# The experts' weights laid out as pieces, two pieces to a tile and to a DMA

## The chip, the cores and the metric

The program runs on one core of one Trainium2 chip. The metric is the device time of one execution in microseconds (us). The kernel before took 1800.74 us, the median of three runs (1800.19 to 1805.48 us).

## What is computed

Three transformer blocks run one after the other on 256 tokens of width 1024, all in float32. The change is in the second layer of the second block, a mixture of experts: a router picks two of eight experts for each token, and each expert is a SwiGLU with a hidden width of 2816.

```python
def expert_block(args):
    xb, e = args
    return (jax.nn.silu(xb @ w1[e]) * (xb @ w3[e])) @ w2[e]
...
contrib = y_sorted * gate_flat[order][:, None].astype(h.dtype)
out = jax.ops.segment_sum(contrib, sorted_token, num_segments=n_tok)
```

Here `w1[e]` and `w3[e]` are 1024 x 2816 and `w2[e]` is 2816 x 1024, so the eight experts hold 277 MB of weights. Every other stage (attention of several kinds, two dense SwiGLUs, a gated mixer, embeddings per layer) also multiplies the activations by weights that are read once from DRAM.

## The kernel before, in words

**Pieces.** Every weight matrix passes through the chip in pieces of 128 partitions by 1024 float32 (512 KB, 4 KB in a partition). `K.load` (L623) takes a raw buffer in turn from the list `s.raws` and issues one DMA on the SP queue (L632). `K.split` (L636) then makes two fp32r tiles of the raw piece: ScalarE copies it to `hi` (L649), and VectorE writes `lo = raw - hi` (L650). TensorE multiplies three times per product (`mm3`, L673): high by high, high by low and low by high (L675 to L677). The raw buffer is free again when L650 has read it. There are four `hi` and four `lo` buffers (`NH`).

**Rows of a piece.** A piece of an expert's `w1` or `w3` is two blocks of 128 rows by 512 columns (rows of 2 KB in DRAM), or, in the last group of an expert, four blocks by 256 columns (rows of 1 KB). A piece of `w2` is 128 rows of 1024 columns (4 KB). An expert has 66 pieces, all eight 528.

**Raw buffers.** All stages share eight raw buffers of 4 KB a partition (`s.wr`, `NR = 8`); some stages (`phase(..., raw=n)`, L526) add some of their own. Stage `block2b` (L1398) has a ring of ten more for its mixer and the experts. For the experts the list of raw buffers is then made 25 long: these 18, the buffer `xw`, four halves of the two tiles Yh and Yl (class `Spare`, L475), `xt`, and one of the four tiles `b4`. One further piece goes once into another `b4` tile (`units.where`).

**Order of the experts.** `Units` (L411) lists all pieces in the order in which they are taken: a group's `w1` and `w3`, then the `w2` of the group before. `Units.ahead` loads a piece early, `Units.fetch` splits the next one (and loads it if it was not loaded), `Units.take` hands it to `experts` (L1590). Pieces 0 to 2 are fetched and 3 to 7 loaded ahead in `gm` (L1444), the stage before; pieces 4 to 7 go to `b4` tiles. In `route`, `experts` and around them the order of TensorE, VectorE and ScalarE is written out by hand (`with s.in_order()`, L546). In the other stages, and on the SP queue, the builder of the program orders the instructions by priorities and by a model of time of its own, so they need not follow the code.

**After the experts.** `moe` (L1535) loads the eight pieces of `ple_gate` into the eight buffers `s.wr`, reads a count, and branches (`tc.If(cnt > P)`, L1545) around a second pass over all experts, which is needed only if an expert has over 128 tokens. In these runs the branch is not taken into the second pass.

Of the kernel before, what the change touches and what calls it, by code (L numbers as in the profile page):

```python
# [9 lines left out]
F32 = mybir.dt.float32  # L10
# [9 lines left out]
P = 128  # L20
D = 1024
NEG = -1.0e30
FF = 2816
NE = 8
# [53 lines left out]
    return pk  # L78


def host_layout(I):

    return {
        "final_gain": I["final_gain"].reshape(1, D),
        "final_norm_2": I["final_norm_2"].reshape(1, D),
        "final_norm_g_3": I["final_norm_g_3"].reshape(1, D),
        "ln_ffn1": I["ln_ffn_2"][1:2],
        "c_ln_g_2": I["c_ln_g_2"].reshape(1, D),
        "c_ln_b_2": I["c_ln_b_2"].reshape(1, D),
        "c_w_sT": np.ascontiguousarray(I["c_w_s_2"][0].transpose(2, 0, 1)),  # L90
        "positions_2": np.ascontiguousarray(I["positions_2"].reshape(2, P).T),
    }
# [86 lines left out]
class NextX:  # L179
# [5 lines left out]
    def __init__(s, k, g, row, tag, width, off):  # L185
        s.k, s.row, s.off = k, row, off
        s.pair = k.x_pair(tag, [P, 8, width])
        s.ssq = k.ts(8)
        if row is None:
            s.g = g  # L190
        else:
            s.grow = k.bcast(row)
            s.g = k.ts(8)
            k.nc.vector.tensor_tensor(out=s.g, in0=k.p(row), in1=g, op=ALU.mult)
# [54 lines left out]
class Last:  # L249
# [7 lines left out]
    def half(s, t):  # L257
# [11 lines left out]
        nc.vector.scalar_tensor_tensor(h[:, t, cs[1]], h[:, t, cs[1]], r, s.grow[:, cs[1]], op0=ALU.mult, op1=ALU.mult)  # L269
        out = k.A["out"].rearrange("(t p) d -> p t d", p=P)  # L270
        for c in cs:
# [139 lines left out]
class Units:  # L411


    def __init__(s, k):
        A = k.A
        s.k, s.early, s.where, s.n, s.loaded, s.ready = k, {}, {}, 0, 0, []
        s.todo = []
        todo2 = []
        for e in range(NE):
            for g0 in range(0, FF // P, 4):  # L420
                n = min(4, FF // P - g0)
                for w in ("moe_w1_2", "moe_w3_2"):
                    s.todo += [(src, kp, n * P, c) for c, src, kp in k.pieces(A[w][0, e], 0, 8, g0 * P, n * P)]
                s.todo += todo2
                todo2 = [(src, kp, D, g0 + c) for c, src, kp in k.pieces(A["moe_w2_2"][0, e], g0, n, 0, D)]
        s.todo += todo2

    def load(s, n, pool=None):
        src, kp, w, _ = s.todo[n]
        s.loaded = max(s.loaded, n + 1)  # L430
        return s.k.load(src, kp, w, None if pool is None else pool.tile([P, D], F32, tag="raw", name=s.k.nm("raw")))

    def ahead(s, n, pool=None):
        s.early[n] = s.load(n, pool)

    def fetch(s):

        if s.n < len(s.todo):
            hi, lo = s.k.split(*(s.early.pop(s.n, None) or s.load(s.n, s.where.get(s.n))))
            _, kp, _, c = s.todo[s.n]  # L440
            s.ready.append([(c + j, hi[:, j], lo[:, j]) for j in range(kp)])
            s.n += 1

# [16 lines left out]
class InTurn:  # L460
# [5 lines left out]
    def tile(s, shape, dt, tag, name):  # L466
        s.pools.append(s.pools.pop(0))
        return s.pools[-1].tile(shape, dt, tag="one", name=name)

    def keep(s):  # L470

        s.pools.pop()


class Spare:  # L475


    def __init__(s, k):
        s.k, s.n = k, 0

    def tile(s, shape, dt, tag, name):
        if s.n % 2 == 0:
            s.t = s.k.xp.tile([P, 2 * D], F32, tag="Y" + "hl"[s.n // 2 % 2], name=name)
        s.n += 1
        return s.t[:, :D] if s.n % 2 else s.t[:, D:]


class K:
    UE = 1024

    def __init__(s, ctx, tc, A):
        s.tc, s.nc, s.A = tc, tc.nc, A
        pool = lambda name, bufs, **kw: ctx.enter_context(tc.tile_pool(name=name, bufs=bufs, **kw))
        nc = s.nc
        s.n = 0
        s.cp = pool("cp", 1)
        s.NR, s.NH = 8, 4
        s.wr, s.wh, s.wl = pool("wr", s.NR), pool("wh", s.NH), pool("wl", s.NH)
        s.xp = pool("xp", 1)

        s.sm = pool("sm", 48)
        s.dp = pool("dp", 1, space=DRAM)
        s.ct, s.chain = {}, (None, {})
        s.h = s.cp.tile([P, 2, D], F32, name="h")
        x = A["x"].rearrange("(t p) d -> p t d", p=P)
        ck = s.cp.tile([P, C_W["ck"]], F32, name="ck")
        s.ct["ck"] = ck
        nc.sync.dma_start(ck[:, :P], A["ck"][:, :P])
        for i in range(2):
            for t in range(2):  # L510
                nc.sync.dma_start(s.h[:, t, 512 * i:512 * i + 512], x[:, t, 512 * i:512 * i + 512])
        s.pk = s.cp.tile([P, PK_2], F32, name="pk")
        nc.sync.dma_start(s.pk[:, :PK_1], A["pk"][:, :PK_1])
        s.ident = s.c("ident")
        s.later = True
# [6 lines left out]
            s.later = False  # L522


    @contextmanager
    def phase(s, name, b8=0, b4=0, b2=0, b1=0, raw=0, hl=0, ring=None, ps=(("mm", 4), ("acc", 2), ("fil", 2)), extra=()):  # L526
        with ExitStack() as st:
            pool = lambda nm, bufs, **kw: st.enter_context(
                s.tc.tile_pool(name=f"{name}_{nm}", bufs=bufs, reuse_waits="tile", **kw))
            s.b8 = pool("b8", b8) if b8 else None  # L530
            s.b4 = pool("b4", b4) if b4 else None
            s.b2 = pool("b2", b2) if b2 else None
            s.b1 = pool("b1", b1) if b1 else None
            s.one = pool("one", 1)
            for nm, bufs in extra:
                setattr(s, nm, pool(nm, bufs))
            mk = lambda base, n, nm, m: [base] * n + ([pool(nm, m)] * m if m else [])
            s.raws, s.his, s.los = mk(s.wr, s.NR, "xr", raw), mk(s.wh, s.NH, "xh", hl), mk(s.wl, s.NH, "xl", hl)
            if ring is not None:
                s.raws = s.raws + [ring[0]] * ring[1]  # L540
            s.nraw = s.nhl = 0
            s.psp = ps if isinstance(ps, dict) else {t: pool(f"ps_{t}", n, space=PSUM) for t, n in ps}
            yield

# [853 lines left out]
    def block2b(s):  # L1398
        with ExitStack() as st:
            pool = lambda nm, bufs, **kw: st.enter_context(s.tc.tile_pool(name="b2b_" + nm, bufs=bufs, **kw))  # L1400
            ring, kp = pool("xr", 10), pool("pp", 1)
            b4 = [pool(f"b4{i}", 1, reuse_waits="tile") for i in range(4)]
            xw, xt = pool("xw", 1), pool("xt", 1)
            keep = lambda shape, dt=F32: kp.tile(shape, dt, name=s.nm("keep"))
            pq = InTurn([pool("pq", 1, reuse_waits="tile")])
            ps = [pool(f"ps{i}", 1, space=PSUM, reuse_waits="tile") for i in range(8)]
            with s.phase("gm", b8=2, b2=2, ring=(ring, 10), ps=dict(mm=InTurn(ps[:4]), acc=InTurn(ps[4:6]), fil=InTurn(ps[6:]))):
                s.b4 = InTurn(b4)
                s.consts("cm", kp)

                nc = s.nc
                nc.gpsimd.memset(keep([P, 72]), 0.0)
                t = xt.tile([P, 4, 256], F32R, tag="raw", name=s.nm("pT"))
                pT = s.ple_in(1, (t[:, 0:2], t[:, 2:4]))
                units, rest, pp = s.gm(pT, pq, keep, xw.tile([P, 8, 128], F32, tag="raw", name=s.nm("wst")))
                at = s.nraw % len(s.raws)
                raws = s.raws[at:] + s.raws[:at] + [xw] + [Spare(s)] * 4 + [xt, InTurn(b4[2:3])]
            with s.phase("moe", b1=3, ps=dict(mm=InTurn(ps[:2]), ab=InTurn(ps[2:6]), acc=InTurn(ps[6:])), extra=(("bx", 4),)):
                s.raws = raws
                s.sh, s.hp, s.yp = [InTurn([b4[i]]) for i in (0, 1, 3)]  # L1420

                units.where = {units.loaded + len(raws): s.yp}
                s.b4 = InTurn(b4)
                nx, pre = s.moe(units, ring, rest)
                s.b4 = InTurn(b4)
                s.x3()
                s.b4 = InTurn(b4[1:])
                s.ple(1, nx, pp, s.x, pre, ("acc", "ab"))
# [566 lines left out]
def build(tc, A, phases):  # L1995
    with ExitStack() as ctx:
        k = K(ctx, tc, A)
        for ph in phases:
# [2 lines left out]

PHASES = ("block1", "block2a", "block2b", "block3")
DIRECT = ("w_in_even", "w_out_even", "w_in_odd", "w_out_odd", "p_2", "a_w_in_2", "a_w_out_2", "ffn_w1_2", "ffn_w3_2",
          "ffn_w2_2", "c_w_in_2", "c_w_out_2", "moe_w1_2", "moe_w3_2", "moe_w2_2", "ple_gate_2", "ple_proj_2",
          "meta_tokens_3", "w_in_3", "w_uq_3", "w_ukv_3", "w_o_3", "w_gate_3", "w_up_3", "w_down_3")


# [22 lines left out]
```

## Time and profile before

| | before |
|---|---|
| three runs | 1800.19, 1800.74, 1805.48 us |
| the profiled execution | 1804.6 us |
| its span, first to last instruction | 1802.8 us |
| mean granted TensorE clock | 0.991 |
| bytes read from DRAM | 443.61 MB |
| experts' DMAs | 528 of 512 KB |

The profiled execution took 1.8 us more than its span, and 3.9 us more than the median of the three runs. An engine is busy while it works on an instruction that is no wait, branch or DMA issue. PE is TensorE's matmuls and PEld its weight loads, DVE is VectorE, ACT ScalarE, POOL GpSimd, SP the engine whose queue issues the DMAs. Matmuls overlap each other in the records, so their distance is read from their starts.

### The profile page before, as it was taken

The page shows a single profiled execution, that of the slowest core. Times are in us where ns is not written, and L with a number is a line of the kernel's source. Part 1 is how long each engine was busy: PE and PEld are TensorE (multiplying, and loading weights), DVE is VectorE, ACT ScalarE, POOL GpSimd, SP SyncE. Part 2 cuts the span into 40 slices and gives each one's busy share as a digit, 9 for nine tenths or more (in the row PEclk, how much of TensorE's full clock was granted, in tenths as well). Part 3 has the DMA queues.
Part 4 walks back from the last instruction along what each step waited for, and adds up shares of the span by engine and source line. Part 5 has one row for each costly group of instructions (what it writes and reads, how often), then busy time and mean ns, then how long its engine had stood idle before and what let it go on. Part 6 is the DMA issues. An engine that isn't in the chain of part 4 may idle for free. (4 is left out here: it accounts for less than half of the span.)

```text
span 1802.8 us, 27631 instructions
## 1 busy us (share of the span) xinstructions
PE 1770.3 (98%) x10129; PEld 1536.7 (85%) x10129; DVE 1389.0 (77%) x2013; ACT 1136.2 (63%) x1566; POOL 92.5 (5%) x102
## 2 busy tenths in 40 slices
PE   8999999999999999999999999999999899999998
PEld 7879879899987888888888888888888688889997
DVE  6676779745466789998989999999999788865544
ACT  6354665644456568777777787777878665554443
POOL 1100010111000110000000000000000020001101
PEclk9899999999999999999999999999999899999999
DMA  8535463866547879999999999999997554357640
GB/s 285 192 118 163 146 193 127 262 183 186 186 139 246 278 249 372 354 365 341 363 366 359 359 344 377 347 379 320 379 355 275 163 161 132 94 191 219 187 130 24
DMA packets 215761, 446.57 MB, mean 248 GB/s; under 512 B 15145, under 2 KB 44081, under 8 KB 215489
## 3 DMA queue, kind: packets, MB, share of 16 engines
q1 hardware_dynamic: 215616, 444.72, 72.5%
q8 instruction: 81, 1.33, 0.3%
q14 instruction: 64, 0.52, 0.1%
HBM read 443.61 MB, written 2.63 MB: 248 GB/s over the span
## 5 line engine op out<-in xcount | busy, mean ns | idle before, releaser
L650 DVE TENSOR_TENSOR lo<-raw,hi 128x1024 fp32r<-128x1024 f32 (+1 forms) x828 | 989.0, 1225 | 303.8 <-ACT hi L649 292.8
L649 ACT CAST hi<-raw 128x1024 fp32r<-128x1024 f32 (+1 forms) x828 | 851.9, 1048 | 443.4 <-PE mm L677 134.0
L675 PE MATMUL ab<-hi,bx 128*128 128x512 f32 (+1 forms) x768 | 290.6, 378 | 0.0
L676 PE MATMUL ab<-hi,bx 128*128 128x512 f32 (+1 forms) x768 | 285.7, 372 | 0.3 <-DVE bx L746 0.3
L677 PE MATMUL ab<-lo,bx 128*128 128x512 f32 (+1 forms) x768 | 286.0, 372 | 0.0
L675 PE MATMUL mm<-Xh,hi 128*128 128x256 f32 x760 | 215.7, 284 | 2.0 <-DVE Xl L749 2.0
L677 PE MATMUL mm<-Xl,hi 128*128 128x256 f32 x760 | 215.4, 283 | 0.0
L676 PE MATMUL mm<-Xh,lo 128*128 128x256 f32 x760 | 215.3, 283 | 0.0
L677 PEld LDWEIGHTS ab<-lo,bx 128*128 128x128 f32 x768 | 144.6, 188 | 25.7
L676 PEld LDWEIGHTS ab<-hi,bx 128*128 128x128 f32 x768 | 144.9, 189 | 24.3 <-DVE bx L746 0.6
L675 PEld LDWEIGHTS ab<-hi,bx 128*128 128x128 f32 x768 | 144.8, 189 | 23.7
L675 PEld LDWEIGHTS mm<-Xh,hi 128*128 128x128 f32 x760 | 146.0, 192 | 3.2 <-ACT hi L649 2.3
L676 PEld LDWEIGHTS mm<-Xh,lo 128*128 128x128 f32 x760 | 146.0, 192 | 0.9 <-DVE lo L650 0.2
L677 PEld LDWEIGHTS mm<-Xl,hi 128*128 128x128 f32 x760 | 146.1, 192 | 0.0
L675 PE MATMUL acc<-hi,hp 128*128 128x512 f32 x352 | 137.3, 390 | 0.0
L676 PE MATMUL acc<-hi,hp 128*128 128x512 f32 x352 | 137.1, 390 | 0.0
L677 PE MATMUL acc<-lo,hp 128*128 128x512 f32 x352 | 137.0, 389 | 0.0
L675 PE MATMUL fil<-Xh,hi 128*128 128x256 f32 (+1 forms) x352 | 102.4, 291 | 1.0 <-ACT b L1919 0.5
L677 PE MATMUL fil<-Xl,hi 128*128 128x256 f32 (+1 forms) x352 | 101.0, 287 | 0.0
L676 PE MATMUL fil<-Xh,lo 128*128 128x256 f32 (+1 forms) x352 | 100.9, 287 | 0.0
L677 PEld LDWEIGHTS acc<-lo,hp 128*128 128x128 f32 x352 | 66.1, 188 | 13.9
L675 PEld LDWEIGHTS acc<-hi,hp 128*128 128x128 f32 x352 | 66.1, 188 | 13.1
(496 smaller groups left out, 2794.3 us busy)
## 6 DMA issues: line engine op xcount, KB each, us to landing
raw<-in_moe_w_dram SPq DMA_DIRECT2D x528, 512.0 KB, 5.9
raw<-in_ffn_w_dram SPq DMA_DIRECT2D x66, 512.0 KB, 3.6
raw<-in_a_w_in_dram SPq DMA_DIRECT2D x24, 512.0 KB, 3.7
raw<-in_w_gate_dram SPq DMA_DIRECT2D x22, 512.0 KB, 3.8
raw<-in_w_up_dram SPq DMA_DIRECT2D x22, 512.0 KB, 3.8
raw<-in_w_down_dram SPq DMA_DIRECT2D x22, 512.0 KB, 3.6
raw<-in_w_in_odd_dram SPq DMA_DIRECT2D x20, 512.0 KB, 3.6
raw<-in_w_in_even_dram SPq DMA_DIRECT2D x18, 512.0 KB, 6.9
```

What stands on the lines that cost most here:

```text
L649: nc.scalar.copy(hi[:, :m], raw[:, :m])
L650: nc.vector.tensor_tensor(out=lo[:, :m], in0=raw[:, :m], in1=hi[:, :m].bitcast(F32), op=ALU.subtract)
L675: nc.tensor.matmul(out, lhsT=lh, rhs=rh, start=start, stop=False, skip_group_check=skip)
L676: nc.tensor.matmul(out, lhsT=ll, rhs=rh, start=False, stop=False, skip_group_check=skip)
L677: nc.tensor.matmul(out, lhsT=lh, rhs=rl, start=False, stop=stop, skip_group_check=skip)
```

## The change

On the host, the three expert tensors become one tensor `moe` of shape (8 experts, 33 tiles, 128, 2048): each tile holds two pieces that are taken one after the other, as the left and right half of 128 rows of 8 KB. Raw buffers become halves of 8 KB buffers (`Halves`, in place of `Spare`): `s.wr` is four of these, the ring of `block2b` five. `Units.load` brings two pieces with one DMA of 1 MB where the piece is a left half, the next buffer is a `Halves`, and the second piece is not placed elsewhere. The list for the experts is now 24 long: the 18, four halves of Yh and Yl, `xw`, `xt`; two pieces go once to `b4` tiles. Each stage begins on a whole 8 KB buffer (`even`). The other weights are still loaded by `K.load`, a piece to a DMA, into the halves.

```diff
+def expert_tiles(I):
+    T = np.empty((NE, FF // P * 3 // 2, P, 2 * D), np.float32)
+    for e in range(NE):
+        n = 0
+        for g0 in range(0, FF // P, 4):
+            c = min(4, FF // P - g0) * P
+            for w in ("moe_w1_2", "moe_w3_2"):
+                a = I[w][0, e][:, g0 * P:g0 * P + c].reshape(-1, 2 * D // c, P, c).transpose(0, 2, 1, 3)
+                T[e, n:n + len(a)] = a.reshape(-1, P, 2 * D)
+                n += len(a)
+            a = I["moe_w2_2"][0, e][g0 * P:g0 * P + c].reshape(-1, 2, P, D).transpose(0, 2, 1, 3)
+            T[e, n:n + len(a)] = a.reshape(-1, P, 2 * D)
+            n += len(a)
+    return T
...
 class Units:
...
-                for w in ("moe_w1_2", "moe_w3_2"):
-                    s.todo += [(src, kp, n * P, c) for c, src, kp in k.pieces(A[w][0, e], 0, 8, g0 * P, n * P)]
+                for i in range(2 * n):
+                    s.todo.append((T[e, u + i // 2], i % 2, 8 // n, n * P, i % n * (8 // n)))
+                u += n
                 s.todo += todo2
-                todo2 = [(src, kp, D, g0 + c) for c, src, kp in k.pieces(A["moe_w2_2"][0, e], g0, n, 0, D)]
+                todo2 = [(T[e, u + i // 2], i % 2, 1, D, g0 + i) for i in range(n)]
+                u += n // 2
...
     def load(s, n, pool=None):
-        src, kp, w, _ = s.todo[n]
+        src, i, kp, w, _ = s.todo[n]
+        k, cs = s.k, slice(i * D, i * D + D)
         s.loaded = max(s.loaded, n + 1)
-        return s.k.load(src, kp, w, None if pool is None else pool.tile([P, D], F32, tag="raw", name=s.k.nm("raw")))
+        if pool is not None:
+            raw = pool.tile([P, D], F32, tag="raw", name=k.nm("raw"))
+            k.nc.sync.dma_start(raw, src[:, cs])
+            return raw, kp, w
+        at = k.raws[k.nraw % len(k.raws)]
+        if i == 0 and isinstance(at, Halves) and n + 1 not in s.early and n + 1 not in s.where:
+            raw = at.both(k.nm("raw"))
+            k.nc.sync.dma_start(raw, src)
+            k.nraw += 2
+            s.loaded = max(s.loaded, n + 2)
+            s.early[n + 1] = (raw[:, D:], *s.todo[n + 1][2:4])
+            return raw[:, :D], kp, w
+        raw = at.tile([P, D], F32, tag="raw", name=k.nm("raw"))
+        k.nraw += 1
+        k.nc.sync.dma_start(raw, src[:, cs])
+        return raw, kp, w
 
     def ahead(s, n, pool=None):
-        s.early[n] = s.load(n, pool)
+        if n not in s.early:
+            s.early[n] = s.load(n, pool)
...
-class Spare:
+class Halves:
-    def __init__(s, k):
-        s.k, s.n = k, 0
+    def __init__(s, make):
+        s.make, s.n = make, 0
     def tile(s, shape, dt, tag, name):
         if s.n % 2 == 0:
-            s.t = s.k.xp.tile([P, 2 * D], F32, tag="Y" + "hl"[s.n // 2 % 2], name=name)
+            s.t = s.make(name)
         s.n += 1
         return s.t[:, :D] if s.n % 2 else s.t[:, D:]
+    def both(s, name):
+        assert s.n % 2 == 0
+        s.n += 2
+        return s.make(name)
+    def even(s):
+        s.n += s.n % 2
...
-        s.wr, s.wh, s.wl = pool("wr", s.NR), pool("wh", s.NH), pool("wl", s.NH)
+        s.wr, s.wh, s.wl = s.halves(pool("wr", s.NR // 2)), pool("wh", s.NH), pool("wl", s.NH)
...
             s.nraw = s.nhl = 0
+            for a in s.raws:
+                if isinstance(a, Halves):
+                    a.even()
...
-            ring, kp = pool("xr", 10), pool("pp", 1)
+            ring, kp = s.halves(pool("xr", 5)), pool("pp", 1)
...
-                raws = s.raws[at:] + s.raws[:at] + [xw] + [Spare(s)] * 4 + [xt, InTurn(b4[2:3])]
+                raws = s.raws[at:] + s.raws[:at] + [s.spare()] * 4 + [xw, xt]
...
-                units.where = {units.loaded + len(raws): s.yp}
+                units.where = {units.loaded + len(raws) + i: p for i, p in enumerate((s.yp, InTurn(b4[2:3])))}
```

## Rows read from the trace of the kernel before

**Rows 1.** The page: busy us of each engine, share of the span, instructions.

```profile
PE 1770.3 (98%) x10129; PEld 1536.7 (85%) x10129; DVE 1389.0 (77%) x2013; ACT 1136.2 (63%) x1566; POOL 92.5 (5%) x102
```

**Rows 2.** Busy time by stretch: a dense SwiGLU, then the experts.

```profile
core 0: us, PE busy (x) PEld busy (x) DVE busy (x) ACT busy (x) POOL busy (x), PEclk, DMA share, GB/s
...
345.00:525.00 180.00, 180.00 (x1277) 169.98 (x1276) 92.76 (x90) 79.98 (x90) 19.89 (x11) 1.00 0.63 195
690.00:1380.00 690.00, 690.00 (x3336) 579.94 (x3335) 637.84 (x625) 539.63 (x591) 0.00 (x0) 1.00 0.99 358
```

**Rows 3.** Groups of TensorE within 690 to 1380 us: busy us, mean ns, idle before.

```profile
L675 PE MATMUL ab<-hi,bx 128*128 128x512 f32 (+1 forms) x685 | 259.4, 379 | 0.0
L676 PE MATMUL ab<-hi,bx 128*128 128x512 f32 (+1 forms) x685 | 255.0, 372 | 0.0
```

**Rows 4.** Matmuls in order of time: start us, us; experts, then the stage behind them.

```profile
903.10 0.39 PE L676 MATMUL acc<-hi,hp 128*128 128x512 f32 x1
903.33 0.39 PE L677 MATMUL acc<-lo,hp 128*128 128x512 f32 x1
...
1441.99 0.39 PE L675 MATMUL acc<-hi,Yh 128*128 128x512 f32 x1
1442.22 0.39 PE L676 MATMUL acc<-hi,Yl 128*128 128x512 f32 x1
```

**Rows 5.** Splitting on VectorE, dense SwiGLU 345 to 525 us, then experts 690 to 1380.

```profile
L650 DVE TENSOR_TENSOR lo<-raw,hi 128x1024 fp32r<-128x1024 f32 x64 | 78.3, 1225 | 83.2 <-ACT hi L649 83.1
...
L650 DVE TENSOR_TENSOR lo<-raw,hi 128x1024 fp32r<-128x1024 f32 x472 | 555.9, 1221 | 42.8 <-ACT hi L649 36.2
```

**Rows 6.** The experts' weight tensors: who waited for their DMAs (us, times), landing times.

```profile
  ACT hi L649: 0.4, 1
  DVE lo L650: 0.2, 1
...
DMA to landing us min/median/max: 3.5/5.9/9.8
```

**Rows 7.** Waits within 690 to 1380 us: us in total, times, longest us.

```profile
ACT hi L649 <- PE acc L676: 49.8, 139, 1.0
...
SPq L632 <- DVE lo L650: 444.6, 409, 3.6
```

**Rows 8.** The two halves of a Yh or Yl tile: SP issues, VectorE frees.

```profile
687.51 0.81 SPq L632 DMA_DIRECT2D raw<-in_moe_w_dram  x2
...
685.13 3.50 DVE L650 TENSOR_TENSOR lo<-raw,hi 128x1024 fp32r<-128x1024 f32 x3 [0.70 <-ACT hi L649]
```

**Rows 9.** The page's DMA issues: count, KB each, median us to landing.

```profile
raw<-in_ffn_w_dram SPq DMA_DIRECT2D x66, 512.0 KB, 3.6
...
raw<-in_w_in_even_dram SPq DMA_DIRECT2D x18, 512.0 KB, 6.9
```

**Rows 10.** TensorE's waits over the whole span, two of 19 kinds: us, times, longest.

```profile
PE mm L805 <- DVE one L809: 1.1, 1, 1.1
...
PE mm L896 <- DMA b<-in_p_dram: 0.8, 1, 0.8
```

**Rows 11.** End of the experts: SP issues, last split, branch records, first work behind.

```profile
1399.16 10.75 SPq L632 DMA_DIRECT2D raw<-in_ple_gate_dram  x8
...
1415.36 1.23 DVE L650 TENSOR_TENSOR lo<-raw,hi 128x1024 fp32r<-128x1024 f32 x1 [0.39 <-ACT hi L649]
...
L1545 SPq EVENT_SEMAPHORE  x8: 17/17/17, 1415.1 to 1415.6; - x8
...
L1545 PEldq COMPARE_BRANCH  x1: 3382/3382/3382, 1423.1 to 1423.1; - x1
...
1426.80 0.63 ACT L214 ACTIVATE b<-h 128x512 f32<-128x512 f32 x1 [6.72 <-DVEq L1545]
```

**Rows 12.** SP issues around 210 to 240 us.

```profile
201.69 6.02 SPq L632 DMA_DIRECT2D raw<-in_a_w_in_dram  x3
208.56 0.37 SPq L1223 DMA_DIRECT2D b<-in_p_dram  x1
```

More of the change, by code (lines that the diff above doesn't have):

```diff
@@ L78, in pack_params @@
     return pk
+def expert_tiles(I):
[12 more added lines that the diff above has]
+    return T
 def host_layout(I):
     return {
+        "moe": expert_tiles(I),
         "final_gain": I["final_gain"].reshape(1, D),
@@ L414, in __init__ @@
     def __init__(s, k):
-        A = k.A
+        T = k.A["moe"]
         s.k, s.early, s.where, s.n, s.loaded, s.ready = k, {}, {}, 0, 0, []
@@ L419, in __init__ @@
         for e in range(NE):
+            u = 0
             for g0 in range(0, FF // P, 4):
                 n = min(4, FF // P - g0)
-                for w in ("moe_w1_2", "moe_w3_2"):
-                    s.todo += [(src, kp, n * P, c) for c, src, kp in k.pieces(A[w][0, e], 0, 8, g0 * P, n * P)]
+                for i in range(2 * n):
+                    s.todo.append((T[e, u + i // 2], i % 2, 8 // n, n * P, i % n * (8 // n)))
+                u += n
                 s.todo += todo2
-                todo2 = [(src, kp, D, g0 + c) for c, src, kp in k.pieces(A["moe_w2_2"][0, e], g0, n, 0, D)]
+                todo2 = [(T[e, u + i // 2], i % 2, 1, D, g0 + i) for i in range(n)]
+                u += n // 2
         s.todo += todo2
     def load(s, n, pool=None):
-        src, kp, w, _ = s.todo[n]
+        src, i, kp, w, _ = s.todo[n]
+        k, cs = s.k, slice(i * D, i * D + D)
         s.loaded = max(s.loaded, n + 1)
-        return s.k.load(src, kp, w, None if pool is None else pool.tile([P, D], F32, tag="raw", name=s.k.nm("raw")))
+        if pool is not None:
[14 more added lines that the diff above has]
+        return raw, kp, w
     def ahead(s, n, pool=None):
-        s.early[n] = s.load(n, pool)
+        if n not in s.early:
+            s.early[n] = s.load(n, pool)
     def fetch(s):
@@ L439, in fetch @@
             hi, lo = s.k.split(*(s.early.pop(s.n, None) or s.load(s.n, s.where.get(s.n))))
-            _, kp, _, c = s.todo[s.n]
+            _, _, kp, _, c = s.todo[s.n]
             s.ready.append([(c + j, hi[:, j], lo[:, j]) for j in range(kp)])
@@ L522, in tables, with halves, spare @@
             s.later = False
+    def halves(s, pool):
+        return Halves(lambda name: pool.tile([P, 2 * D], F32, tag="raw", name=name))
+    def spare(s):
+        return Halves(lambda name: s.xp.tile([P, 2 * D], F32, tag="Y" + "hl"[s.n % 2], name=name))
     @contextmanager
@@ L2003 @@
 DIRECT = ("w_in_even", "w_out_even", "w_in_odd", "w_out_odd", "p_2", "a_w_in_2", "a_w_out_2", "ffn_w1_2", "ffn_w3_2",
-          "ffn_w2_2", "c_w_in_2", "c_w_out_2", "moe_w1_2", "moe_w3_2", "moe_w2_2", "ple_gate_2", "ple_proj_2",
+          "ffn_w2_2", "c_w_in_2", "c_w_out_2", "ple_gate_2", "ple_proj_2",
           "meta_tokens_3", "w_in_3", "w_uq_3", "w_ukv_3", "w_o_3", "w_gate_3", "w_up_3", "w_down_3")
```

## The prediction

> **What bounds the kernel now.** I read the busy times first. TensorE is busy 1770.3 us of the 1802.8 us span [rows 1], so all its idle time is 32.5 us, and no change that leaves its work alone can win more. The change touches no matmul. Next I took the stretch of the experts alone, 690 to 1380 us: the DMA engines are busy 0.99 of it at 358 GB/s, which looks like a limit, but TensorE is busy 690.00 of 690.00 us at a granted clock of 1.00, its level of 2.4 GHz [rows 2], and its groups there show an idle time of 0.0 [rows 3]. "Busy" can hide a slow matmul, so I read starts in order of time: among the experts they lie 0.23 us apart, and in the stage behind them again 0.23 us [rows 4]. The loads do not slow the matmuls. The splitting agrees with that: 1221 ns for a VectorE split among the experts, 1225 ns in a dense SwiGLU at 195 GB/s [rows 2, 5]. Last I looked for who waits for a load. In all 528 loads of the experts ScalarE waited once for 0.4 us and VectorE once for 0.2 us [rows 6]; otherwise ScalarE waits for TensorE to give back `hi` buffers (the largest such row is 49.8 us), and SP waits 444.6 us for raw buffers that VectorE frees [rows 7]. So the order of dependence is: TensorE sets the pace, splitting follows it, loading follows splitting.
>
> **The experts' loads.** 528 DMAs become 288. The list is 24 long with `xw` and `xt` at its end: 518 pieces go round it (528 less pieces 0 to 3, 4 to 7 and the two of `where`), 21 full rounds use both single buffers, so 42 single loads, and six more go to `b4`; the other 480 pieces are 240 pairs. Their cost today is the 0.6 us of waits [rows 6]; I take 0, bounds -0.6 and 0. What hides them is the lead. 472 pieces are split in 690 us [rows 5], one in 1.46 us. A load now waits for the buffer used 25 pieces earlier, so it is issued about 24 pieces, 35 us, ahead of its use, and lands within 9.8 us [rows 6]. After the change the left half of a pair waits until both old halves are free, about 22 pieces or 32 us ahead. If a 1 MB load took twice the longest landing seen, 19.6 us, some 12 us would still be left. Fewer issues shorten SP's work, but SP waits for buffers most of this stretch [rows 7], so that is worth 0.
>
> Can the second half of a tile be loaded while the first is read? The halves of Yh and Yl show it: when VectorE had freed two halves at 687.5 us, SP issued two loads, both within 0.81 us [rows 8]. The first had to wait for both old halves, the second did not wait for the first to be split. This is the behaviour I assume for all raw buffers.
>
> By the Trainium skill, "DMA: Bandwidth & Descriptors", section "Measured (HBM→SBUF, 128 partitions, SWDGE, issued from GpSimd)", one should batch to 1 MiB or more, since 1 MB moves at 341 GB/s and 64 KB at 138; from its fit (2.0 us plus bytes over 436e3) an estimate is 6.4 us for two loads of 512 KB and 4.4 us for one of 1 MB, 480 us over 240 pairs if loads ran one at a time (the page's loads came from another queue, GpSimd's). The trace does not agree that 512 KB is slow in a stream: 358 GB/s on average [rows 2]. The sum stays at 0 by the rows.
>
> **The other stages.** Eight buffers become four pairs, so every second load is issued one piece later; in a dense SwiGLU a piece takes 180 us over 64, 2.8 us, so the lead falls from about eight pieces to seven, 20 us, against a landing of 3.6 us [rows 5, 9]. In the first 60 us, loads land in 6.9 us [rows 9]; seven pieces at the 1.2 us that a VectorE split alone takes [rows 5] are 8.4 us, so it holds, narrowly. I take 0, with an upper bound of 2 us: two late pairs at about half their lost lead each.
>
> **A load queued behind.** TensorE waits 0.8 us once for a small load of `in_p` [rows 10]. It is queued on SP directly behind a raw load. If that one is issued as the right half of a pair, 0.4 us (half of the 0.81 us for two issues [rows 8]) after the left one, `in_p` goes out that much later. I take +0.4 us; the bounds are -0.8 us (the wait disappears) and +2.8 us (a whole piece later).
>
> **The end of the experts.** The eight loads of `ple_gate` go into `s.wr`. With 25 buffers these held pieces 515 to 522; with 24 they hold pieces 520 to 527, the very last, because 518 loads end in place 13 of the list, which is the last of the eight. So SP issues them not from 1399.16 to 1409.9 us but until the last split has ended, 1416.6 us [rows 11], and passes the branch 7 us later. Behind it SP waits for these loads to land: 1415.6 us before [rows 11]; 1417.0 plus 3.6 to 9.8 us now [rows 6, 9], so 1420.6 to 1426.8 us. TensorE's own branch ends at 1423.1 plus 3.38, 1426.5 us, and the other engines start at 1426.80 us [rows 11]. I take 0, near the lower landing time since few loads run by then; the upper bound is +0.3 us.
>
> **The sum.** 0 + 0 + 0.4 + 0 = +0.4 us on the profiled 1804.6 us, 1805.0 us. That execution lies 3.9 us above the median of the runs shown; on the median of 1800.7 us it makes 1801.1 us. All bounds together reach from -1.4 to +5.1 us. A difference under 0.3%, 5.4 us, is what a measurement of this kernel can hardly tell from none.
>
> **Rivals.**
>
> *The loads do limit the experts (faster).* For it: a DMA share of 0.99 [rows 2], and the first matmul of a product takes 379 ns on average where the second takes 372 [rows 3], 7 ns by 685, 4.8 us, that might be late pieces. Against it: the leads above and 0.6 us of waits. If true: 4.8 + 0.6 us less, 1795.3 us. This is also where the rule of the Trainium skill on batching would show.
>
> *The builder orders the other stages anew.* For it: only the router and the experts have their order written out, and elsewhere the order is not the code's: `in_p` stands first in its stage, but SP issued it behind three loads of `in_a_w_in` [rows 12]. Later and fewer loads can shift attention and norms against each other. Place: the stages outside the experts. Price: a typical new stall is like the 1.1 us of L805 [rows 10]; it decides from five such stalls on (5.4 over 1.1). With seven, +7.7 us, 1808.8 us. Against it: the loads there have leads that the pairs hardly touch. The same shuffle could remove stalls, but there are only 32.5 us of idle time, some of them at the start and the end; five removed would give 1795.6 us.
>
> *Pairs are not formed.* If pieces and buffers fell out of step, each half would come by its own DMA with rows of 4 KB. Nothing waits for them either way: 1801 us. The counts of loads before the experts (16, 8, 2 and two pairs) are even, which speaks against it.
>
> **Chances.** Forecast (nothing that can be told) 0.67, pairs not formed 0.04; loads limit 0.06; new order slower 0.16, new order faster 0.07. Faster is 0.06 + 0.07 = 0.13, slower 0.16, same 0.71. The forecast's own bounds are 1799.3 to 1805.8 us (1800.7 less 1.4, plus 5.1); the range takes in both results of a new order, 1794.5 to 1809 us.
>
> **What the profile would show.** Right: about 288 experts' DMAs, most of 1024 KB; TensorE still busy without a gap from 690 to 1380 us; a lower DMA share there at the same GB/s; `ple_gate` issued until about 1417 us, and ScalarE starting behind the branch near 1426.8 us; TensorE's wait for `in_p` near 1.2 us. Wrong: ScalarE or TensorE waiting for `raw` anywhere, matmul starts among the experts that are not 0.23 us apart, or a changed order of matmuls in attention with new waits of a microsecond.

## The result, and the profile after

The changed kernel takes **1851.45 us** (median of four runs, 1845.71 to 1857.41) against 1803.11 us (four runs, 1800.19 to 1806.78) before: a ratio of 1.0271 [1.025, 1.0292], 48 us slower. The prediction was 1801.1 us, range 1794.5 to 1809. It was wrong.

The page's line for busy time, against [rows 1]:

```profile
PE 1787.4 (97%) x10129; PEld 1543.0 (83%) x10129; DVE 1386.2 (75%) x2013; ACT 1135.5 (61%) x1566; POOL 94.5 (5%) x102
```

The counts of instructions are those of before, so no work was added to an engine. The span grew from 1802.8 to 1849.3 us, TensorE's busy time by 17 us; the rest is idle time. Where it lies, the same stretches tell as in [rows 2] (columns as there):

```profile
345.00:525.00 180.00, 180.00 (x1274) 169.75 (x1273) 92.47 (x90) 80.11 (x91) 19.90 (x11) 1.00 0.58 190
690.00:1380.00 690.00, 667.88 (x3176) 555.46 (x3175) 604.37 (x593) 511.18 (x562) 0.00 (x0) 0.99 0.87 339
```

The dense SwiGLU is as it was. Among the experts TensorE, which had no gap, is now idle for 22 of 690 us, and the loads bring 339 GB/s in place of 358. So it is not a lack of DMA speed: the DMA engines have more free time, 0.87 busy against 0.99. The groups of TensorE there, against [rows 3], say who makes it wait:

```profile
L734 PE MATMUL ab<-hi,bx 128*128 128x512 f32 (+1 forms) x654 | 249.2, 381 | 9.8 <-ACT hi L708 9.8
...
L734 PE MATMUL acc<-hi,hp 128*128 128x512 f32 x296 | 117.3, 396 | 9.5 <-ACT hi L708 9.5
```

The first matmul of a product waits for `hi`, ScalarE's copy of the raw piece. (The lines moved: L708 and L709 are L649 and L650 of before, L734 to L736 are L675 to L677.) The next question is what ScalarE waits for. The experts' tensor, against [rows 6]:

```profile
L463 SPq DMA_DIRECT2D raw<-in_moe_dram x240: 327/328/779, 587.8 to 1430.2; - x120
L470 SPq DMA_DIRECT2D raw<-in_moe_dram x42: 327/328/983, 604.7 to 1401.9; - x42
L458 SPq DMA_DIRECT2D raw<-in_moe_dram x6: 328/328/341, 583.2 to 656.5; - x6
...
  ACT hi L708: 53.3, 12
...
DMA to landing us min/median/max: 3.6/7.2/17.9
```

240 pairs and 48 single loads, as foreseen, but ScalarE waits for them 12 times, 53.3 us in all, where it waited 0.4 us once. Two of the twelve are short. The other ten last 4.5 to 7.2 us each, and stand in front of pieces 102, 126, 150, 222, 246, 366, 390, 414, 486 and 510: all distances are multiples of 24, the length of the list of raw buffers. One place of the list is at fault, and not in every round.

**One stall from close by**, the first, at piece 102. First SP, in three stretches: 776.9 to 781, then 781 to 790.2, in which it issued nothing, then 790.2 to 793.5 (start, us, issues):

```profile
777.11 3.41 SPq L463 DMA_DIRECT2D raw<-in_moe_dram  x2
...
790.27 2.58 SPq L463 DMA_DIRECT2D raw<-in_moe_dram  x5
```

SP's waits from 776 to 796 us (in total, times, longest):

```profile
SPq L463 <- DVE lo L709: 14.8, 3, 9.7
```

Then VectorE, ScalarE and TensorE around it, in order of time:

```profile
784.15 6.10 DVE L709 TENSOR_TENSOR lo<-raw,hi 128x1024 fp32r<-128x1024 f32 x5
...
789.96 0.59 ACT L804 CAST hp<-mm 128x512 fp32r<-128x512 f32 x1 [0.97 <-PE mm L1678]
795.38 2.94 ACT L708 CAST hi<-raw 128x1024 fp32r<-128x1024 f32 x3 [4.83 <-DMA raw<-in_moe_dram]
...
793.64 0.39 PE L736 MATMUL ab<-lo,bx 128*128 128x512 f32 x1
796.48 0.50 PE L734 MATMUL ab<-hi,bx 128*128 128x512 f32 x1 [2.45 <-ACT hi L708]
```

SP waited 9.7 us for a split on VectorE, which ended at 784.15 + 6.10 = 790.25 us; at 790.27 the load went out, with four more at once behind it. ScalarE starts on it at 795.38 us, after an idle time of 4.83 us, and TensorE, which lives on the split pieces in the four `hi` and `lo` buffers for a while, loses 2.45 us. So the load of this piece was issued when the piece *just ahead of it* had been split, one piece ahead and not 22. While SP stood there, the DMA engines ran nearly dry, and then full (busy time and granted clock by stretch, columns as in [rows 2]):

```profile
785.00:790.00 5.00, 5.00 (x26) 4.15 (x24) 4.84 (x5) 3.21 (x4) 0.00 (x0) 1.00 0.19 79
790.00:797.00 7.00, 4.55 (x20) 3.30 (x18) 1.48 (x3) 2.17 (x3) 0.00 (x0) 0.99 0.78 301
797.00:804.00 7.00, 6.63 (x23) 5.14 (x23) 6.74 (x7) 5.91 (x7) 0.00 (x0) 0.76 1.01 422
```

**The line behind it.** The diff above leaves out how the list's four Y halves are made. Before, `Spare` took Yh and Yl by a counter of its own. The changed kernel has this (L577):

```diff
-            s.t = s.k.xp.tile([P, 2 * D], F32, tag="Y" + "hl"[s.n // 2 % 2], name=name)
+    def spare(s):
+        return Halves(lambda name: s.xp.tile([P, 2 * D], F32, tag="Y" + "hl"[s.n % 2], name=name))
```

In `Spare`, `s` was the `Spare`, and `s.n` its count of halves. In the lambda `s` is `K`, and `K.n` is the count of all names given to tiles so far. Whether a pair gets Yh or Yl is the parity of that count. The list holds two such pairs, one behind the other, at places 18, 19 and 20, 21. Worked out from the program, the two take the same tile in rounds 4, 5, 6, 9, 10, 15, 16, 17, 20 and 21 of 21. In these rounds the second pair can be loaded only when the first one, two pieces ahead, has been read. Place 20 of these ten rounds holds exactly the ten pieces above.

**The account.** The first instruction behind the branch, against [rows 11]:

```profile
1470.48 0.63 ACT L234 ACTIVATE b<-h 128x512 f32<-128x512 f32 x1 [7.04 <-DVEq L1604]
```

It starts at 1470.48 us, 43.7 us later than before; of the 46.5 us of longer span 2.8 us lie behind it. The experts can also be measured without the other stages: from the start of ScalarE's copy of piece 26 to the start of the experts' last matmul it is 740.6 us before (681.88 to 1422.51) and 785.2 us now (680.65 to 1465.88), 44.6 us more. This is called the experts' own time below. Worked out from the starts of all matmuls there: 32 distances of over 0.46 us (twice the usual one) that before does not have make 36 us over the usual, and 32 of 0.38 to 0.46 us, near the 0.43 us of the lower clock (last section), make another 6 us, together 42 of the 44.6 us.

### The profile page after: what moved, and what is told of

Same layout as the page of the kernel before. It is cut to its first block, busy times and chain, and to the rows that moved or that the text cites. A ratio compares the mean times of both kernels' runs of the same rounds, so it can differ in the third digit from the quotient of the medians.

```text
span 1849.3 us, 26920 instructions
## 1 busy us (share of the span) xinstructions
PE 1787.4 (97%) x10129; PEld 1543.0 (83%) x10129; DVE 1386.2 (75%) x2013; ACT 1135.5 (61%) x1566; POOL 94.5 (5%) x102
## 5 line engine op out<-in xcount | busy, mean ns | idle before, releaser
L709 DVE TENSOR_TENSOR lo<-raw,hi 128x1024 fp32r<-128x1024 f32 (+1 forms) x828 | 986.9, 1221 | 354.1 <-ACT hi L708 342.8
L708 ACT CAST hi<-raw 128x1024 fp32r<-128x1024 f32 (+1 forms) x828 | 850.6, 1047 | 495.2 <-PE mm L736 133.8
L734 PE MATMUL ab<-hi,bx 128*128 128x512 f32 (+1 forms) x768 | 294.0, 383 | 14.9 <-ACT hi L708 14.9
L736 PE MATMUL ab<-lo,bx 128*128 128x512 f32 (+1 forms) x768 | 289.5, 377 | 1.9 <-DVE lo L709 1.8
L735 PE MATMUL ab<-hi,bx 128*128 128x512 f32 (+1 forms) x768 | 288.3, 375 | 0.2 <-DVE bx L805 0.2
L734 PE MATMUL mm<-Xh,hi 128*128 128x256 f32 x760 | 215.7, 284 | 2.0 <-DVE Xl L808 2.0
L736 PE MATMUL mm<-Xl,hi 128*128 128x256 f32 x760 | 215.4, 283 | 0.0
L734 PEld LDWEIGHTS ab<-hi,bx 128*128 128x128 f32 x768 | 146.5, 191 | 41.0 <-ACT hi L708 17.4
L736 PEld LDWEIGHTS ab<-lo,bx 128*128 128x128 f32 x768 | 146.3, 190 | 31.4 <-DVE lo L709 5.4
L734 PEld LDWEIGHTS mm<-Xh,hi 128*128 128x128 f32 x760 | 146.0, 192 | 3.1 <-ACT hi L708 2.3
L734 PE MATMUL acc<-hi,hp 128*128 128x512 f32 x352 | 139.3, 396 | 9.5 <-ACT hi L708 9.5
L736 PEld LDWEIGHTS mm<-Xl,hi 128*128 128x128 f32 x760 | 146.0, 192 | 0.0
L736 PE MATMUL acc<-lo,hp 128*128 128x512 f32 x352 | 139.2, 395 | 1.2 <-DVE lo L709 1.2
L734 PE MATMUL fil<-Xh,hi 128*128 128x256 f32 (+1 forms) x352 | 102.4, 291 | 1.0 <-ACT b L1978 0.5
L736 PE MATMUL fil<-Xl,hi 128*128 128x256 f32 (+1 forms) x352 | 100.9, 287 | 0.0
L734 PEld LDWEIGHTS acc<-hi,hp 128*128 128x128 f32 x352 | 67.0, 190 | 23.8 <-ACT hi L708 10.8
L736 PEld LDWEIGHTS acc<-lo,hp 128*128 128x128 f32 x352 | 66.9, 190 | 17.8 <-DVE lo L709 4.0
```

Of the source, the lines that this page charges most:

```text
L708: nc.scalar.copy(hi[:, :m], raw[:, :m])
L709: nc.vector.tensor_tensor(out=lo[:, :m], in0=raw[:, :m], in1=hi[:, :m].bitcast(F32), op=ALU.subtract)
L734: nc.tensor.matmul(out, lhsT=lh, rhs=rh, start=start, stop=False, skip_group_check=skip)
L735: nc.tensor.matmul(out, lhsT=ll, rhs=rh, start=False, stop=False, skip_group_check=skip)
L736: nc.tensor.matmul(out, lhsT=lh, rhs=rl, start=False, stop=stop, skip_group_check=skip)
```

## The experiments

**Theory:** the loads are late only because both Y pairs of a round fall on one tile. **Rivals:** a load of 1 MB in rows of 8 KB, or the binding of two pieces to each other, makes the leads too short by itself; or the builder's order of other stages lost the time.

**e1_turn**: the changed kernel with Yh and Yl strictly in turn.

```diff
-        return Halves(lambda name: s.xp.tile([P, 2 * D], F32, tag="Y" + "hl"[s.n % 2], name=name))
+        turn = [0]
+        def make(name):
+            turn[0] += 1
+            return s.xp.tile([P, 2 * D], F32, tag="Y" + "hl"[turn[0] % 2], name=name)
+        return Halves(make)
```

> The changed kernel, but the two Y tiles are taken strictly in turn by a counter of their own. Theory (in 10 of 21 rounds of the buffer list both pairs of a round got the same Y tile, so that the second pair could be asked for only when the first had been split): the 10 stalls of ScalarE at every 24th piece go (53.3 us of waits on raw to under 1 us), time 1803 us, between 1798 and 1808. Rival A (loads of 1 MB, or a list of 24 with pairs, come too late as such): the stalls stay, 1845 to 1857 us. Rival B (the builder's order of the other stages): the 48 us stay outside the experts, over 1840 us.

Measured: 1806.02 us (12 runs) against 1801.37 us (29 runs), 1.0012 [0.9998, 1.0026]. The experts' tensor and the stretch of the experts (L714 is the line that was L708):

```profile
  ACT hi L714: 0.9, 3
...
DMA to landing us min/median/max: 3.6/7.0/10.5
```

```profile
690.00:1380.00 690.00, 690.00 (x3335) 579.96 (x3334) 638.44 (x625) 539.05 (x591) 0.00 (x0) 1.00 0.94 358
```

All ten stalls are gone and with them some 45 of the 48 us, while the 240 pairs, the 8 KB rows and the buffers are the same. The experts' own time is 740.6 us, as before. This is the cause, shown by taking it away. The longest landing fell from 17.9 to 10.5 us; the two longest of the changed kernel, 17.9 and 16.3 us, belong to loads that went out at 1204.2 and 1240.4 us, in the crowds behind the late loads of pieces 366 and 390.

**e2_one_tile**: the opposite, both pairs on Yh in every round.

```diff
-        return Halves(lambda name: s.xp.tile([P, 2 * D], F32, tag="Y" + "hl"[s.n % 2], name=name))
+        return Halves(lambda name: s.xp.tile([P, 2 * D], F32, tag="Yh", name=name))
```

> The changed kernel, but every pair that goes to the Y tiles takes Yh. Theory: a stall in each of the 21 rounds, 48.3 us over 10 is 4.8 us each, 21 times 4.8 is 101 us, 1904 us (1885 to 1920). Rival A: as the changed kernel, about 1851 us. Rival B: about 1851 us.

Measured: 1937.44 us (2 runs), 1.0744 [1.0712, 1.0776]. There are 21 long stalls, the first at piece 28 and the others at 54, 78, 102 and so on to 510, one in each round. Their number is as the theory has it; their price is not. 136 us over 21 is 6.5 us each, where the changed kernel gave 48 over 10, 4.8 us (by the experts' own time, 868.4 us, it is 6.1 against 4.5). The waits, and the stretch of the experts:

```profile
ACT hi L708 <- DMA raw<-in_moe_dram: 134.7, 23, 9.4
...
PE acc L734 <- ACT hi L708: 41.1, 12, 5.0
PE ab L734 <- ACT hi L708: 29.1, 10, 6.3
```

```profile
690.00:1380.00 690.00, 628.93 (x2845) 513.52 (x2846) 546.45 (x536) 458.63 (x506) 0.00 (x0) 0.94 0.82 304
```

A stall is longer (up to 9.4 us on ScalarE, 7.2 in the changed kernel), and the granted clock is 0.94 here against 0.99: from the starts of matmuls, 72 distances of over 0.46 us make 96 us over the usual, and 134 near that of the lower clock 27 us. The load that ended a stall took up to 7.8 us to land where that can be read, at most 5.0 us in the changed kernel. Why a stall grows when one follows in each round was not tried.

**b1_one_tile**: the same fault in the kernel *before*, with its 528 single loads, so without a load of 1 MB.

```diff
-            s.t = s.k.xp.tile([P, 2 * D], F32, tag="Y" + "hl"[s.n // 2 % 2], name=name)
+            s.t = s.k.xp.tile([P, 2 * D], F32, tag="Yh", name=name)
```

> The kernel before (loads of 512 KB, no pairs), but its four halves of Y tiles are all taken from Yh. Theory (a tile that is asked for twice in one round of the list costs a stall, whatever the size of the load): 20 stalls in 20 rounds; per stall 6.5 us (136 us over 21 of e2_one_tile) less about 1 us, since a load of 512 KB lands in 3.5 us where 1 MB takes 4.6; 20 times 5.4 is 108 us, 1909 us (1890 to 1930). Rival (the stalls need the pairs and their 1 MB): within 10 us of 1802.

Measured: 1890.43 us (2 runs) against 1804.88 us (25 runs), 1.0482 [1.0453, 1.051]. ScalarE's row:

```profile
ACT hi L649 <- DMA raw<-in_moe_w_dram: 100.9, 34, 7.0
```

Twenty long stalls, at pieces 29, 55, 80 and from there every 25th to 505: one a round, 25 being the length of this list (two of them the profile puts down to TensorE and not to the load). So the fault needs neither the binding of two pieces nor a load of 1 MB. 86 us over 20 is 4.3 us each, less than the 5.4 us forecast, and the time is at the very edge of the range. The price does differ: with the fault in every round as here, pairs cost 6.5 us each (e2_one_tile), though the changed kernel's 4.8 us is near. A load that ended a stall landed in 3.5 to 4.4 us here, in 4.7 to 5.0 us in the changed kernel, where that can be read.

**e4_no_spare**: the changed kernel without the four Y halves, a list of 20.

```diff
-                raws = s.raws[at:] + s.raws[:at] + [s.spare()] * 4 + [xw, xt]
+                raws = s.raws[at:] + s.raws[:at] + [xw, xt]
```

> The changed kernel without the Y tiles in the list: 20 buffers long instead of 24, pairs as they are. Theory: no tile is shared, a lead of some 18 pieces times 1.46 us, 26 us, against loads that land in 7.2 us, so the stalls go: 1803 us, 1798 to 1808. Rival A: a shorter list makes loads still later, over 1851 us. Rival B: about 1851 us.

Measured: 1803.87 us (10 runs), 1.0008 [0.9995, 1.0022]; ScalarE waits 2.9 us in five times, and the experts' own time is 740.6 us. Four buffers fewer do no harm; four that share one tile in ten rounds cost 48 us.

**e3_turn_single**: e1_turn with a DMA of 512 KB for each half, rows of 4 KB.

```diff
-        if i == 0 and isinstance(at, Halves) and n + 1 not in s.early and n + 1 not in s.where:
+        if False:
```

> As e1_turn, but no pairs are formed: each half is brought by a DMA of its own (512 KB, rows of 4 KB), 528 DMAs instead of 288. Theory: loads have over 20 us in hand, so the time is that of e1_turn within 3 us. Rival A: if 1 MB loads are late as such, this one is faster than e1_turn by over 5 us; if large loads help, slower by over 5 us.

Measured: 1802.01 us (12 runs), 0.9994 [0.998, 1.0008]; ScalarE waits 1.2 us in four times, and the experts' own time is again 740.6 us. It is 4.0 us faster than e1_turn, not within 3 us as expected, and short of the 5 us named for rival A. The experts do not show the difference (see "What stays open"). So 528 issues cost the experts nothing, and pairs gain nothing.

**Eight buffers instead of 24.** If the lead is what hides the loads, how much of it is needed? Three kernels with the list cut to the eight of `s.wr`: s8_pair is the changed kernel (no Y tile is left in the list), s8_single is e3_turn_single, s8_before is the kernel before.

```diff
-                raws = s.raws[at:] + s.raws[:at] + [s.spare()] * 4 + [xw, xt]
+                raws = [s.wr] * 8
```

> The changed kernel with a list of 8 buffers (the four 8 KB buffers that all stages share) for the experts, pairs of 1 MB. Theory (only the lead counts): the left half of a pair is issued seven pieces before its use, 7 times 1.36 us less 2.3 us for the split itself, 7.2 us, against a median landing of 7.0 us: on the edge, 0 to 40 us slower than e1_turn, and slower than s8_single. Rival (1 MB loads with rows of 8 KB bring more per us, by the batching rule): the fastest of the three lists of 8.

> As s8_pair, but each half by a DMA of its own (512 KB, rows of 4 KB). Theory: issued eight pieces ahead, 8 times 1.36 us less 2.3, 8.6 us, and landing is nearer 4 to 6 us with fewer bytes in flight: 0 to 10 us slower than e3_turn_single. Rival (batching): slower than s8_pair.

> The kernel before with a list of its 8 shared buffers alone for the experts: loads of 512 KB with rows of 1, 2 or 4 KB. Theory: as s8_single within 10 us if the row length matters little; the rows of 1 KB in the last group of each expert may add up to a few us per expert. Rival (short rows limit the supply, which is what the layout is for): over 20 us slower than s8_single.

Measured, against the same 25 runs of the kernel before (1804.88 us): s8_pair 1808.69 us, 1.002 [1.0004, 1.0036]; s8_single 1800.85 us, 0.9993 [0.9978, 1.0008]; s8_before 1803.03 us, 0.9997 [0.9982, 1.0013] (ten runs each). The three times came out as the theory has it, and neither rival did: pairs are the slowest of the three, not the fastest, and short rows cost nothing that could be told. In s8_pair ScalarE's own row looks worse than in the changed kernel, but TensorE's busy time does not:

```profile
ACT hi L708 <- DMA raw<-in_moe_dram: 67.5, 76, 3.5
```

```profile
690.00:1380.00 690.00, 687.30 (x3308) 573.66 (x3308) 628.93 (x619) 528.41 (x586) 0.00 (x0) 1.00 0.95 356
```

67.5 us in 76 waits of up to 3.5 us cost 2.7 us of TensorE's busy time here, and the experts' own time is 746.6 us, 6.0 us longer; in the changed kernel 53.3 us in 12 waits, ten of them over 4.5 us, cost 22 us of busy time and 44.6 us of the experts' own time. The four `hi` and `lo` buffers bridge part of a wait (of 4.83 us at piece 102 TensorE lost 2.45), so many short waits cost far less than a few long ones of the same sum. In s8_single and s8_before that time is 740.6 us, and in s8_before ScalarE waits for none of the 528 loads, in rows of 1 to 4 KB. For single loads the 17 further buffers and their long lead buy nothing here; with pairs, the longer list saves the 6.0 us.

**What stays open.** In both comparisons on one chip the pairs came out slower than the single loads, by 4.0 us (e1_turn, e3_turn_single) and 7.8 us (s8_pair, s8_single) of the medians; the intervals against before just overlap, but that of s8_pair lies above 1. With eight buffers most of it is found: the 6.0 us in the experts. With the long list the experts take 740.6 us either way, so the 4.0 us lie in other stages. In the two profiled executions 3.7 us of it lie behind the experts' last matmul (383.9 us to the end against 380.2), but s8_single, without pairs, has 382.6 us there. One thing differs in sight: behind the branch, ScalarE's first two `ACTIVATE` instructions of L234 (L214 of before) lie 1.6 us apart, with an instruction of the next step between them, in all five kernels with pairs, and 0.6 us in before, e3_turn_single, s8_single and s8_before. It does not come from the pairs alone, as b1_one_tile, without pairs, has the 1.6 us too. It moves the first `ple_gate` matmul by less than 1 us: this starts 6.3 to 6.4 us after ScalarE's first instruction where they lie 1.6 us apart, and 5.5 to 5.7 us after it in the others. The rest was not tried. None of these kernels is faster than the one before by what could be told.

## Why the prediction was wrong, step by step

**The step that failed** is the lead in the part on the experts' loads: "After the change the left half of a pair waits until both old halves are free, about 22 pieces or 32 us ahead." It took the list to be 24 *different* places. In ten of 21 rounds two pairs of places were one tile, and the lead there was one piece. The counting of rounds and places was done, but the Y tiles' turn was carried over from [rows 8], which show the kernel before. "This is the behaviour I assume for all raw buffers" passed over the one part of them whose turn the change rewrote: `Spare`'s counter. With that line read, the cost could have been bounded from the rows at hand: a landing of 3.5 to 9.8 us [rows 6] against one piece of 1.46 us [rows 5], ten times, is 20 to 83 us before what the split buffers bridge. The experts measured 44.6 us longer where the sum has 0.

**The sign named for "wrong" was the one that showed:** ScalarE waits for `raw`. None of the rivals had this cause. The one on the slow side (a new order in other stages) would have given the right sign for a wrong reason: the stages behind the experts grew by 2.8 us, and the loads of the experts began no later than before (583.2 us).

**What held**, mostly seen in e1_turn, where the fault is away:
- TensorE sets the pace and the DMA share near 0.99 was no limit: 690.00 of 690.00 us busy, the share 0.94 at the same 358 GB/s.
- 240 pairs and 48 single loads; in e1_turn the experts' loads land after 7.0 us (median) and 10.5 us at most, where 19.6 us was assumed at worst. With the stalls the longest came near it, 17.9 us.
- The rival that loads limit the experts falls. It would have shown as a gain, and e1_turn has none: its experts take the 740.6 us of before. By the Trainium skill, "DMA: Bandwidth & Descriptors", section "Measured (HBM→SBUF, 128 partitions, SWDGE, issued from GpSimd)", DMAs are to be batched to 1 MiB or more, for 75% of peak bandwidth or more. Here, with the loads hidden and issued by SP, 1 MB gained no time over 512 KB: 1.0012 in e1_turn against 0.9994 in e3_turn_single, and s8_before, with 512 KB, has 0.9997.
- The dense SwiGLU keeps TensorE busy for 180.00 of 180.00 us.
- The end of the experts: `ple_gate` was issued until 1460.9 us (1450.33 + 10.53), 0.9 us behind the last split's end (1458.72 + 1.23), and landed in 5.5 us at most. ScalarE starts behind the branch after 7.04 us of idle time, 6.72 before (6.76 in e1_turn). The term was 0, with an upper bound of 0.3 us.
- `in_p`: TensorE's wait fell from 0.8 to 0.2 us, where +0.4 us was forecast. SP issued it right behind raw loads, as before, 0.3 us later (234.41 against 234.09 us), and TensorE waited less, so the delay of the issue did not decide the wait; what did was not tried. The wait is 0.6 us in e1_turn, and 0.4 us in s8_before, which has no pairs. The bounds held. A new wait of 1.1 us came at L403, in the router; s8_single, without pairs, has it too. So the rival of a new order showed on the scale of one such wait, not seven.

TensorE's two rows for these, of its waits over the whole span:

```profile
PE mm L403 <- DVE keep L398: 1.1, 1, 1.1
...
PE mm L955 <- DMA b<-in_p_dram: 0.2, 1, 0.2
```

## What to carry to other kernels

When a change rewrites who hands out buffers, write down which buffer each turn gets, over several rounds, before costing anything: a list's length is a lead only if its places are different buffers. Where a queue issues in order, one buffer that is late holds back every load behind it, however many of those have their buffers free (here SP issued nothing for 9 us, then five loads at once). And do not price waits by their sum: here 67.5 us of short waits cost 6 us, and 53.3 us with ten long ones among them cost 44.6 us.

## What was not expected of the hardware

After the 2.45 us gap TensorE did not come back at once at full speed. Its starts in order of time (changed kernel):

```profile
798.33 0.63 PE L734 MATMUL ab<-hi,bx 128*128 128x512 f32 x1
798.76 0.63 PE L735 MATMUL ab<-hi,bx 128*128 128x512 f32 x1
...
800.40 0.39 PE L736 MATMUL ab<-lo,bx 128*128 128x512 f32 x1
800.63 0.39 PE L734 MATMUL ab<-hi,bx 128*128 128x512 f32 x1
```

0.43 us apart, then 0.23 again; the stretch from 797 to 804 us has a granted clock of 0.76 with TensorE busy for 6.63 of 7 us. The engine was at the level of 2.4 GHz before the gap, and at 1.2 GHz for a few matmuls behind it. The same came behind eight of the ten stalls, and the length of TensorE's gap does not tell them apart: behind a gap of 1.97 us the clock stayed at 1.00, behind one of 1.94 us it fell.

```profile
834.60:841.60 7.00, 6.47 (x35) 5.34 (x36) 7.00 (x9) 5.92 (x8) 0.00 (x0) 1.00 1.02 423
1243.89:1250.89 7.00, 6.84 (x30) 5.44 (x31) 7.00 (x9) 4.87 (x7) 0.00 (x0) 0.76 1.00 421
```

A stall of a few microseconds can thus cost more than its length: some 6 us over the ten stalls here, 27 us in e2_one_tile.
